# Attention scores in three 64-row passes, two heads side by side in the array

## The chip, the cores and the metric

The kernel runs on one core of a Trainium2 chip. The metric is the device time in microseconds of one execution. Three executions of the kernel before took 2763.01, 2763.8 and 2765.96 us; the median is 2763.8 us.

## What is computed

One layer of a hybrid encoder trunk over 2048 tokens of width 1024, in fp32. The input is normalised and projected; three mixers run in parallel on the projection (chunked attention with 6 heads of 64, a causal depthwise convolution, a retention with 6 heads of 64); their outputs are projected and added, and a squared-ReLU MLP and a gated per-layer embedding follow. The change touches the attention scores:

```python
q = rmsnorm(to_chunk_heads(q, H_ATT), qn_g)
k = rmsnorm(to_chunk_heads(k, H_ATT), kn_g)
...
scores = jnp.einsum('bhncd,bhnkd->bhnck', q, kb).astype(jnp.float32) * (d ** -0.5)
scores = scores + bias[None, :, None]
scores = jnp.where(valid[None, None, :, None, :], scores, -1e30)
probs = jax.nn.softmax(scores, axis=-1).astype(v.dtype)
out = jnp.einsum('bhnck,bhnkd->bhncd', probs, vb)
```

Each query chunk of 64 sees its own chunk and the 8 before it.

## The kernel before

The tokens go through in four blocks of 512 (`T`), block by block through all stages. The weight products run in `float32r`, each operand split into a high part (rounded copy, made by ACT) and a low part (the rest, made by DVE); a product is three matmuls, high x high, high x low, low x high (`mm3s`, L173). Transposes and the smaller products of attention and retention are plain fp32 matmuls.

The order of PE's work is the program's order (`keep_in_program_order`, L54 and L59). It is made by a planner at build time. The main stream is a list of segments (L787 on): convolution projection, gate of the block before, then for each of three head pairs an attention projection (`ap`, 96 matmuls of 384 columns) and a retention projection (`rp`, 96 matmuls of 512 columns), then the output projection (`wo_a`, `wo_b`) and the MLP. `posn` counts the main stream. Into it, `advance` (L844) inserts two chains of side work. Chain 0 holds `att_mix(p)` for each head pair, which begins at a fraction `AS` of `rp` of its pair (L835); chain 1 holds `conv_mix` and `ret_mix(p)`. A chain's step may say for how long PE shall do other work before the next step; that is measured on `clk`, a model of PE time that `PE.matmul` adds up, and the amounts stand in `W` (L261): after the q/k transposes `qk`, after the scores `st`, after the transposes of the scores `ts`. The order on the other engines is set by a scheduler from priorities.

`att_mix(p)` (L428) is run 12 times, once for each block and head pair:

- 8 transposes put q and k of the pair into the PSUM tile `qkT`: 128 rows (two heads of 64) by 512 tokens, for q and for k (L437). They read `an`, the normalised rows that POOL writes (L416) at the end of the attention projection.
- The split (L438 to L447). For each head, q is copied by ACT twice: once as the high part into that head's 64 rows of `q[h]`, once more into the other 64 rows; DVE writes the low part into 64 rows of `qlz[h]`, whose other rows are zero. For k, ACT writes the high part into the head's rows of `k[h]` and DVE the low part into the other rows. That is six ACT and four DVE operations of 64x512.
- `scores(t, h)` (L458) for each tile `t` of 128 queries and head `h`: with q high in both halves and k high and low in the halves, one matmul over 128 rows gives high x high + high x low, and a second with `qlz` gives low x high. The keys lie in two segments, this block's (`k`, 128(t+1) columns) and the block before's (`kprev`, the remaining columns up to 640; block 0 has none). The result `sc` is one of two PSUM buffers of tag `s` (`sb2`, L105). DVE adds the bias and takes the maximum (L472), ACT the exponential (L474).
- `trans` (L478) transposes the probabilities back into the same `sc` buffer; ACT (head 0, L484) and DVE (head 1, L486) copy them out as `pT`, which frees the buffer for the next scores.
- `values` (L489) multiplies with v, the two heads writing 64 output rows each of `po` (L495): PE's stationary operand has 64 columns there.

`both(t)` (L500) issues the scores of both heads; it is called once before the tile loop and then after each tile's transposes. `ret_proj` (L535) evacuates each of its four accumulators with four ACT copies (L550 to L554), and two accumulators (`accb`, L102) alternate. `ret_mix` ends with the transposes `roT` (L637).

Of the kernel before, what the change touches and what calls it, by code (L numbers as in the profile page):

```python
# [12 lines left out]
F32R = mybir.dt.float32r  # L13
AF = mybir.ActivationFunctionType
ALU = mybir.AluOpType
AX = mybir.AxisListType

P = 128
D = 1024
S = 2048  # L20
T = 512
# [3 lines left out]
HD = 64  # L25
# [15 lines left out]
def trunk(ctx, tc, a, out):  # L41
    nc = tc.nc
    V, A, G = nc.vector, nc.scalar, nc.gpsimd
    clk, posn = [0.0], [0.0]

    class PE:
        @staticmethod
        def matmul(o, x, y, start, stop):
            n = y.shape[-1]
            if y.dtype == F32R:  # L50
                clk[0] += max(n, 240) / 2200.0
            else:
                clk[0] += max(4 * n * x.shape[-1] / P, 240) / 2200.0
            tc.keep_in_program_order(nc.tensor.matmul(o, x, y, start=start, stop=stop))  # L54
# [12 lines left out]
    def ctile(name, shape, src=None, dt=F32):  # L67
        t = cpool.tile(shape, dt, tag=name, name=name)
        if src is not None:
            nc.sync.dma_start(t, src)  # L70
        return t

    def stile(tag, bufs, shape, name=None, dt=F32):
        return sp.tile(list(shape), dt, tag=tag, name=name or tag, bufs=bufs)
# [16 lines left out]
    def tmp(name, n):  # L91
        return stile("t", 4, [P, n], name)

    def kv(name, shape=(P, 512), dt=F32):
        return stile("kv", 17, shape, name, dt)
# [9 lines left out]
    def sb2(name):  # L105
        return ps.tile([P, 1024], F32, tag="s", name=name, bufs=2)
# [8 lines left out]
    def pob(name):  # L115
        return ps.tile([P, T], F32, tag="po", name=name, bufs=1)

    def f(t):
        return t.bitcast(F32)
# [81 lines left out]
    def split_tr(b, hi, lo, scale):  # L201
        A.activation(hi, b, AF.Copy, scale=scale)
        V.scalar_tensor_tensor(lo, b, scale, f(hi), ALU.mult, ALU.subtract)
# [54 lines left out]
        A.activation(r, b[:, :T], AF.Copy)  # L258

    cur = {}  # L260
    W = dict(qk=6.0, st=4.5, ts=2.0, vo=1.6, r0=3.5, r1=2.4, r2=1.8, r3=11, c1=3.5, c2=2.6, c3=0.6)  # L261

    def xnorm(blk):
        xh, xl = big("xh", 0), big("xl", 1)
# [87 lines left out]
    def conv_mix():  # L352
# [3 lines left out]
        for u in range(2):  # L356
# [13 lines left out]
            for i in range(2):  # L370
                V.tensor_scalar(z[u][:, i * DC : i * DC + DC], b2[:, i], s6[:, 12 + 2 * i : 13 + 2 * i],
                                s6[:, 18 + i : 19 + i], ALU.subtract, ALU.mult)
            yield W["c1"]
        hl = []
        for c in range(2):
# [7 lines left out]
            hl.append((yh, yl))  # L383
            yield W["c2"]
        yield W["c3"]
        for c in range(2):
# [8 lines left out]
            V.scalar_tensor_tensor(ml[:, c], b, bias, f(mh[:, c]), ALU.add, ALU.subtract)  # L395
            yield W["c2"]

# [25 lines left out]
    def mix():  # L423
        if "m" not in cur:
            cur["m"] = big("mh", 2), big("ml", 3)
        return cur["m"]

    def att_mix(p):  # L428
        nats, v = cur["an", p], cur["v", p]
        kprev, vprev = kvc[p]  # L430
        hs = slice(0, HD), slice(HD, P)
        q = [kv("q", dt=F32R) for _ in range(2)]
        k = [kv("k", dt=F32R) for _ in range(2)]
        b = sb2("qkT")
        for j in range(2):
            for t in range(NT):
                PE.transpose(b[:, j * T + t * P : j * T + t * P + P], nats[t][:, j * P : j * P + P], ident)  # L437
        for j, gain in enumerate((qg, kg)):  # L438
            for h in range(2):
                x, y = hs[h], hs[1 - h]  # L440
                bj = b[x, j * T : j * T + T]
                hi = (q, k)[j][h][x]
                A.activation(hi, bj, AF.Copy, scale=gain[x, 0:1])
                lo = qlz[h][x] if j == 0 else k[h][y]
                V.scalar_tensor_tensor(lo, bj, gain[x, 0:1], f(hi), ALU.mult, ALU.subtract)  # L445
                if j == 0:
                    A.activation(q[h][y], bj, AF.Copy, scale=gain[x, 0:1])  # L447
        yield W["qk"]
        rs = stile("rs", 2, [P, 16])
        bias = []  # L450
        for h in range(2):
            bt = stile("bias", 2, [P, 640])
            with tc.high_priority(offset=200):
                nc.sync.dma_start(bt, a["bias"][2 * p + h])
            bias.append(bt)
        po = pob("po")

        def scores(t, h):  # L458
            x = slice(t * P, t * P + P)
            s = sb2("sc")  # L460
            c0 = t * P if kprev is not None else 512
            c1 = 512 + (t + 1) * P
            segs = [(k, 0, 512, c1 - 512)]
            if kprev is not None:
                segs.append((kprev, c0, c0, 512 - c0))
            for kk, ko, so, n in segs:
                PE.matmul(s[:, so : so + n], q[h][:, x], kk[h][:, ko : ko + n], start=True, stop=False)
                PE.matmul(s[:, so : so + n], qlz[h][:, x], kk[h][:, ko : ko + n], start=False, stop=True)
            n = c1 - c0
            pt = tmp("pt", 640)  # L470
            nm = stile("nm", 3, [P, 1])
            V.tensor_tensor_reduce(pt[:, :n], s[:, c0:c1], bias[h][:, 640 - n :], -1.0, 3e38,  # L472
                                   ALU.add, ALU.min, nm[:, 0:1])
            A.activation(pt[:, :n], pt[:, :n], AF.Exp, bias=nm[:, 0:1], scale=-1.0,  # L474
                         accum_out=rs[:, 2 * t + h : 2 * t + h + 1])
            return s, pt, c0 // P, n // P

        def trans(t, h, s, pt, g0, nch):  # L478
            n = nch * P
            for c in range(nch):  # L480
                PE.transpose(s[:, c * P : c * P + P], pt[:, c * P : c * P + P], ident)
            pT = tmp("pT", 640)
            if h == 0:
                A.activation(pT[:, :n], s[:, :n], AF.Copy)  # L484
            else:
                V.tensor_copy(pT[:, :n], s[:, :n])  # L486
            return pT

        def values(t, pT, g0, nch):  # L489
            for c in range(nch):  # L490
                g = g0 + c
                vv = vprev[:, g] if g < 4 else v[:, g - 4]
                for h in range(2):
                    hr = slice(h * HD, h * HD + HD)
                    PE.matmul(po[hr, t * P : t * P + P], vv[:, hr], pT[h][:, c * P : c * P + P],  # L495
                              start=(c == 0), stop=(c == nch - 1))

        sc = {}

        def both(t):  # L500
            for h in range(2):
                sc[h] = scores(t, h)
            return clk[0] + W["st"]

        rdy = both(0)
        pT = span = None
        for t in range(NT):
            yield rdy - clk[0]
            if t:
                values(t - 1, pT, *span)  # L510
            pT = [trans(t, h, *sc[h]) for h in range(2)]
            span = sc[0][2:]
            yield W["ts"]
            if t < NT - 1:
                rdy = both(t + 1)
        V.reciprocal(rs[:, 8:16], rs[:, 0:8])
        rb = tmp("rb", T).rearrange("p (t n) -> p t n", n=P)
        V.tensor_copy(rb.rearrange("p t (h d) -> p (t h) d", d=HD),
                      rs[:, 8:16].unsqueeze(2).to_broadcast([P, 8, HD]))
        yield W["vo"]  # L520
        b = sb2("rT")
        for i in range(NT):
            PE.transpose(b[:, i * P : i * P + P], rb[:, i], ident)
        rT = tmp("rT", T)
        A.activation(rT, b[:, :T], AF.Copy)
        values(NT - 1, pT, *span)
        yield 0
        kvc[p] = k, v
        mh, ml = mix()
        V.tensor_tensor(rT, po, rT, ALU.mult)  # L530
        A.activation(mh[:, AT[p]], rT, AF.Copy)
        V.tensor_tensor(ml[:, AT[p]], rT, f(mh[:, AT[p]]), ALU.subtract)
        yield 0
# [244 lines left out]
    segs, start = [], {}  # L778
# [24 lines left out]
        seg(("gate", NB - 1, half), lambda half=half: gate(NB - 1, half), cP + 8 * cost(512))  # L803

    tasks = []
    AS, RS, RT0, CS, CE, RE, LE, LF, NE, NF, GE, GF, AS0, CS0, CE0 = 0.25, 0.35, 0.03, 0.4, 0.5, 0.95, 0.4, 0.7, 0.4, 0.55, 0.16, 0.22, 0.25, 0.5, 0.5

    def at(name, frac):
        s, c = start[name]
# [73 lines left out]
    for c in range(2):  # L883
        with tc.high_priority(offset=AHEAD):
            next(first)
        x = slice(c * HALF, c * HALF + HALF)
# [13 lines left out]
    qg = ctile("qg", [P, 1], a["qn_g"])  # L900
    V.tensor_scalar(qg, qg, HD ** -0.5, None, ALU.mult)
    kg = ctile("kg", [P, 1], a["kn_g"])
# [7 lines left out]
    G.memset(hist, 0.0)  # L910
    qz = ctile("qz", [P, NT, 2, P])
    G.memset(qz, 0.0)
    qlz = [ctile(f"qlz{h}", [P, T], dt=F32R) for h in range(2)]
    for h in range(2):
        G.memset(f(qlz[h])[HD - h * HD : P - h * HD], 0.0)
    st = []
    for p in range(NPAIR):
        st.append([ctile(f"st{p}{i}", [P, P]) for i in range(2)])
# [100 lines left out]
```

## Time and profile before

| | before |
|---|---|
| median of 3 runs | 2763.8 us |
| profiled execution, its own time | 2768.22 us |
| its span, first to last instruction | 2766.4 us |
| mean granted TensorE clock | 0.990 |
| PE busy | 2683.5 us, 97% |
| DVE busy | 1344.3 us, 49% |
| ACT busy | 745.3 us, 27% |
| POOL busy | 717.6 us, 26% |

The durations come from one profiled execution, 4.4 us above the median. PE is the matmul row; PEld are the loads of the stationary operand. A matmul's own duration is longer than the distance to the next one's start, since matmuls are pipelined; the pace of PE is read from start to start. The granted clock is that of TensorE as a share of 2.4 GHz; it is 1.00 or 0.50.

### The profile page before, as it was taken

The numbers are of one execution on the slowest core, as the hardware profiler recorded it, in microseconds if no ns is written. First come the engines' busy times: TensorE is split into PE (matmuls) and PEld (weight loads), VectorE is DVE, ScalarE is ACT, GpSimd is POOL, SyncE is SP. The second block draws the span as 40 slices with busy tenths as digits, with TensorE's granted clock in tenths as the row PEclk, the third lists the DMA queues.
The fourth block names the chain that finished last, engine by engine and source line by source line (L and its number), as shares of the span: only waits on it lengthen the run. The fifth ranks groups of instructions, "written<-read, shape, count | busy, mean of one in ns | idle before, by whom it ended". The sixth has DMA issues, their size and how long they took to land.

```text
span 2766.4 us, 34253 instructions
## 1 busy us (share of the span) xinstructions
PE 2683.5 (97%) x13178; PEld 2236.1 (81%) x13178; DVE 1344.3 (49%) x2297; ACT 745.3 (27%) x1506; POOL 717.6 (26%) x676
## 2 busy tenths in 40 slices
PE   7899999999899999999999999999999999999999
PEld 6777788887788888888888888888887888888887
DVE  5966655457745543334664554222376555322222
ACT  4454322234144321112324432000122442100011
POOL 4334534334312231222322213001022221210112
PEclk9999999999999999999999999999999999999999
DMA  7647664656633566767663345555655344555554
GB/s 270 237 146 259 230 215 170 208 176 219 206 121 128 193 212 231 259 222 261 240 208 116 132 156 210 187 194 195 231 191 178 117 151 160 190 192 189 197 195 147
DMA packets 123281, 535.35 MB, mean 194 GB/s; under 512 B 12784, under 2 KB 38128, under 8 KB 77040
## 3 DMA queue, kind: packets, MB, share of 16 engines
q1 hardware_dynamic: 123120, 533.17, 54.7%
q8 instruction: 104, 1.70, 0.3%
q14 instruction: 57, 0.47, 0.1%
HBM read 412.54 MB, written 120.59 MB: 193 GB/s over the span
## 4 chain that ended last, share of the span: by engine, by line
PE 82%; DVE 8%; DMA 4%; ACT 2%; issue 2%; POOL 1%; SPq 0%; DVEq 0%; ACTq 0%; POOLq 0%
PE acc L54 46%; PE w L54 26%; DVE y L340 4%; PE po L54 2%; PE sc L54 2%; PE sc L59 2%; DMA w<-k_wr 1%; PE rout L54 1%; DVE w L127 1%; PE ple L54 1%; PE rsc L54 1%; DMA w<-k_wa 1%; DVE k L445 1%; ACT q L447 0%; DMA raw<-in_wc_dram 0%
## 5 line engine op out<-in xcount | busy, mean ns | idle before, releaser
L54 PE MATMUL acc<-xh,w 128*128 128x512 f32 (+1 forms) x1744 | 549.1, 391 | 8.3 <-DVE gate L768 4.0
L54 PE MATMUL acc<-w,xh 128*128 128x512 f32 (+1 forms) x1536 | 469.0, 380 | 18.0 <-DMA w<-k_wa 6.7
L54 PEld LDWEIGHTS acc<-xh,w 128*128 128x128 f32 x1744 | 327.0, 188 | 80.0 <-issue 5.2
L54 PE MATMUL acc<-hid,w 128*128 128x512 f32 x1536 | 367.0, 392 | 0.0
L54 PE MATMUL w<-hid,w 128*128 128x512 f32 x1536 | 362.0, 391 | 0.0
L54 PEld LDWEIGHTS acc<-hid,w 128*128 128x128 f32 x1536 | 288.4, 188 | 63.6
L54 PEld LDWEIGHTS w<-hid,w 128*128 128x128 f32 x1536 | 288.5, 188 | 63.1
L54 PEld LDWEIGHTS acc<-w,xh 128*128 128x128 f32 x1536 | 287.8, 194 | 61.1 <-DMA w<-k_wr 9.5
L54 PE MATMUL acc<-xl,w 128*128 128x512 f32 (+1 forms) x872 | 335.0, 389 | 0.9 <-DVE xl L234 0.9
L54 PE MATMUL w<-xh,w 128*128 128x512 f32 x1024 | 322.0, 390 | 0.0
L127 POOL TENSOR_TENSOR w<-raw,w 128x512 fp32r<-128x512 f32 (+1 forms) x141 | 186.7, 1325 | 506.3 <-ACT w L126 486.6
L692 POOL TENSOR_TENSOR s<-r 128x512 f32<-128x512 f32 x128 | 157.7, 1233 | 554.9 <-DVE r L691 554.9
L126 ACT ACTIVATE w<-raw 128x512 fp32r<-128x512 f32 (+1 forms) x284 | 160.9, 614 | 498.1 <-PE acc L54 279.6
L54 PE MATMUL acc<-w,xl 128*128 128x384 f32 (+1 forms) x768 | 289.2, 377 | 0.0
L693 ACT ACTIVATE hid<-r 128x512 fp32r<-128x512 f32 x128 | 80.2, 628 | 576.3 <-DVE r L691 576.3
L54 PEld LDWEIGHTS w<-xh,w 128*128 128x128 f32 x1024 | 191.9, 188 | 39.7
L127 DVE TENSOR_TENSOR w<-raw,w 128x512 fp32r<-128x512 f32 (+1 forms) x143 | 180.5, 1263 | 81.9 <-ACT w L126 76.7
L340 DVE SCALAR_TENSOR_TENSOR y<-gl,cw,y 128x512 f32<-128x512 f32 x240 | 207.4, 893 | 2.5
L54 PE MATMUL w<-xl,w 128*128 128x512 f32 x512 | 199.2, 389 | 0.0
L54 PEld LDWEIGHTS acc<-xl,w 128*128 128x128 f32 x872 | 164.2, 188 | 36.1 <-DVE xl L234 1.3
L718 DVE TENSOR_TENSOR h<-h,w 128x512 f32<-128x512 f32 x128 | 87.9, 688 | 197.4 <-PE w L54 196.6
L718 DVE TENSOR_TENSOR h<-h,acc 128x512 f32<-128x512 f32 x128 | 87.8, 687 | 173.3 <-PE acc L54 172.8
(182 smaller groups left out, 3291.2 us busy)
## 6 DMA issues: line engine op xcount, KB each, us to landing
w<-k_w SPq DMA_DIRECT2D x160, 1024.0 KB, 4.8
k_w<-w SPq DMA_DIRECT2D x64, 1024.0 KB, 6.8
raw<-in_w_dram SPq DMA_DIRECT2D x96, 512.0 KB, 4.5
w<-k_wr SPq DMA_DIRECT2D x36, 1024.0 KB, 5.9
w<-k_w_g SPq DMA_DIRECT2D x30, 1024.0 KB, 4.8
w<-k_wa SPq DMA_DIRECT2D x36, 768.0 KB, 6.0
w<-k_w_oa SPq DMA_DIRECT2D x18, 1024.0 KB, 6.1
k_wr<-w SPq DMA_DIRECT2D x12, 1024.0 KB, 7.0
```

Source lines behind the costliest of these rows:

```text
L54: tc.keep_in_program_order(nc.tensor.matmul(o, x, y, start=start, stop=stop))
L59: tc.keep_in_program_order(nc.tensor.transpose(o, x, i))
L126: A.activation(w[:, 0, :n], x, AF.Copy)
L127: eng.tensor_tensor(w[:, 1, :n], x, f(w[:, 0, :n]), ALU.subtract)
L340: V.scalar_tensor_tensor(y, gl[:, j : j + T], cw[:, c, j : j + 1], y, ALU.mult, ALU.add)
L445: V.scalar_tensor_tensor(lo, bj, gain[x, 0:1], f(hi), ALU.mult, ALU.subtract)
L692: G.tensor_tensor(s, r, r, ALU.mult)
L693: A.activation(hid[:, j], r, AF.Square)
L718: V.tensor_tensor(h[j], h[j], b, ALU.add)
```

## The change

q and k each become two tiles of all 128 rows, high and low, with head 0 in rows 0 to 63 and head 1 in rows 64 to 127. One ACT copy and one DVE subtraction of 128x512 make each pair (`split_tr`). Scores of both heads are issued together: for each segment three passes, high x high, high x low, low x high, each pass one 64-row matmul for head 0 and one for head 1, into two score buffers. `qlz` and its memsets go. The planner counts a 64-row matmul as half, waits 5.0 in place of 6.0 after the q/k transposes, and begins the attention chain at 0.4 of `rp` in place of 0.25.

```diff
             if y.dtype == F32R:
-                clk[0] += max(n, 240) / 2200.0
+                clk[0] += max(n, 240) / 2200.0 * x.shape[0] / P
...
-    W = dict(qk=6.0, st=4.5, ts=2.0, vo=1.6, r0=3.5, r1=2.4, r2=1.8, r3=11, c1=3.5, c2=2.6, c3=0.6)
+    W = dict(qk=5.0, st=4.5, ts=2.0, vo=1.6, r0=3.5, r1=2.4, r2=1.8, r3=11, c1=3.5, c2=2.6, c3=0.6)
...
-        for j, gain in enumerate((qg, kg)):
-            for h in range(2):
-                x, y = hs[h], hs[1 - h]
-                bj = b[x, j * T : j * T + T]
-                hi = (q, k)[j][h][x]
-                A.activation(hi, bj, AF.Copy, scale=gain[x, 0:1])
-                lo = qlz[h][x] if j == 0 else k[h][y]
-                V.scalar_tensor_tensor(lo, bj, gain[x, 0:1], f(hi), ALU.mult, ALU.subtract)
-                if j == 0:
-                    A.activation(q[h][y], bj, AF.Copy, scale=gain[x, 0:1])
+        for j, (x, gain) in enumerate(((q, qg), (k, kg))):
+            split_tr(b[:, j * T : j * T + T], x[0], x[1], gain[:, 0:1])
...
-        def scores(t, h):
+        def scores(t):
             x = slice(t * P, t * P + P)
-            s = sb2("sc")
+            ss = [sb2("sc") for _ in range(2)]
...
             for kk, ko, so, n in segs:
-                PE.matmul(s[:, so : so + n], q[h][:, x], kk[h][:, ko : ko + n], start=True, stop=False)
-                PE.matmul(s[:, so : so + n], qlz[h][:, x], kk[h][:, ko : ko + n], start=False, stop=True)
+                for i, (a_, b_) in enumerate(((0, 0), (0, 1), (1, 0))):
+                    for h in range(2):
+                        PE.matmul(ss[h][:, so : so + n], q[a_][hs[h], x], kk[b_][hs[h], ko : ko + n],
+                                  start=(i == 0), stop=(i == 2))
             n = c1 - c0
-            pt = tmp("pt", 640)
...
+            out = []
+            for h, s in enumerate(ss):
+                pt = tmp("pt", 640)
...
+                out.append((s, pt, c0 // P, n // P))
+            return out
...
         def both(t):
-            for h in range(2):
-                sc[h] = scores(t, h)
+            sc[:] = scores(t)
             return clk[0] + W["st"]
...
-    AS, RS, RT0, CS, CE, RE, LE, LF, NE, NF, GE, GF, AS0, CS0, CE0 = 0.25, 0.35, 0.03, 0.4, 0.5, 0.95, 0.4, 0.7, 0.4, 0.55, 0.16, 0.22, 0.25, 0.5, 0.5
+    AS, RS, RT0, CS, CE, RE, LE, LF, NE, NF, GE, GF, AS0, CS0, CE0 = 0.4, 0.35, 0.03, 0.4, 0.5, 0.95, 0.4, 0.7, 0.4, 0.55, 0.16, 0.22, 0.4, 0.5, 0.5
...
-    qlz = [ctile(f"qlz{h}", [P, T], dt=F32R) for h in range(2)]
-    for h in range(2):
-        G.memset(f(qlz[h])[HD - h * HD : P - h * HD], 0.0)
```

The function that the split now calls:

```python
def split_tr(b, hi, lo, scale):
    A.activation(hi, b, AF.Copy, scale=scale)
    V.scalar_tensor_tensor(lo, b, scale, f(hi), ALU.mult, ALU.subtract)
```

How the order moves, in block 1, second head pair. PE before, the end of the work behind the q/k transposes and the first scores of tile 0 (24 matmuls `acc` and the four `roT` stand between `qkT` and the first `sc`):

```order
L59 MATMUL qkT<-ident,an 128x128 x8
L59 MATMUL roT<-ident,ro 128x128 x4
L54 MATMUL acc<-w,xh 128x512
L54 MATMUL acc<-w,xl 128x512
...
L54 MATMUL acc<-w,xh 128x512
L54 MATMUL sc<-k,q 128x128
L54 MATMUL sc<-k,qlz_199 128x128
L54 MATMUL sc<-k,q 128x512
L54 MATMUL sc<-k,qlz_199 128x512
L54 MATMUL sc<-k,q 128x128
```

PE now, the same place (22 matmuls `acc` between `qkT` and `sc`):

```order
L59 MATMUL roT<-ident,ro 128x128 x4
L54 MATMUL acc<-w,xh 128x512
L54 MATMUL acc<-w,xl 128x512
L59 MATMUL qkT<-ident,an 128x128 x8
...
L54 MATMUL acc<-w,xh 128x512
L54 MATMUL sc<-k,q 128x128 x6
L54 MATMUL sc<-k,q 128x512 x6
L54 MATMUL acc<-w,xh 128x512
```

The q/k transposes now stand behind the retention's `roT`, and six matmuls over both heads stand where each head had two of its own.

DVE before, the same head pair, from the first low part of q to the first bias-and-maximum of the scores:

```order
L445 SCALAR_TENSOR_TENSOR qlz_199<-qkT,qg,q 64x512
L203 SCALAR_TENSOR_TENSOR ml<-roT,gng,mh 128x512
L445 SCALAR_TENSOR_TENSOR qlz_200<-qkT,qg,q 64x512
L558 TENSOR_TENSOR rb<-rqk,cs 128x4x32
L559 TENSOR_TENSOR rb<-rqk,cs 128x4x32
L560 TENSOR_TENSOR rn<-rqk,cs 128x256
L445 SCALAR_TENSOR_TENSOR k<-qkT,kg,k 64x512
L565 TENSOR_SCALAR e<-e 128x128
L566 RECIPROCAL e<-e 128x128
L445 SCALAR_TENSOR_TENSOR k<-qkT,kg,k 64x512
L472 ISA pt,nm<-sc,bias 128x640
```

DVE now, the same place:

```order
L203 SCALAR_TENSOR_TENSOR ml<-roT,gng,mh 128x512
L203 SCALAR_TENSOR_TENSOR q<-qkT,qg,q 128x512
L203 SCALAR_TENSOR_TENSOR k<-qkT,kg,k 128x512
L554 TENSOR_TENSOR rb<-rqk,cs 128x4x32
L555 TENSOR_TENSOR rb<-rqk,cs 128x4x32
L556 TENSOR_TENSOR rn<-rqk,cs 128x256
L561 TENSOR_SCALAR e<-e 128x128
L562 RECIPROCAL e<-e 128x128
L468 ISA pt,nm<-sc,bias 128x640
```

Two splits stand one behind the other, and the retention's operations (L554 to L562, before L558 to L566) come behind them.

ACT before, the same place:

```order
L443 ACTIVATE q<-qkT,qg 64x512
L202 ACTIVATE mh<-roT,gng 128x512
L447 ACTIVATE q<-qkT,qg 64x512
L443 ACTIVATE q<-qkT,qg 64x512
L550 ACTIVATE rqk<-acc,xss 128x256
L553 ACTIVATE rn<-acc,xss 128x64 x2
L554 ACTIVATE rn<-acc,xss 128x128
L447 ACTIVATE q<-qkT,qg 64x512
L443 ACTIVATE k<-qkT,kg 64x512
L564 ACTIVATE e<-rn 128x128
L443 ACTIVATE k<-qkT,kg 64x512
```

ACT now:

```order
L560 ACTIVATE e<-rn 128x128
L202 ACTIVATE mh<-roT,gng 128x512
L202 ACTIVATE q<-qkT,qg 128x512
L202 ACTIVATE k<-qkT,kg 128x512
L546 ACTIVATE rqk<-acc,xss 128x256
L549 ACTIVATE rn<-acc,xss 128x64 x2
```

The evacuation of a retention accumulator (`rqk`, `rn`) stood between the copies of q and k; now both copies stand between two evacuations.

## Rows read from the trace of the kernel before

**Rows 1.** The page, part 1: busy us (share of the span) and instructions by engine.
```profile
PE 2683.5 (97%) x13178; PEld 2236.1 (81%) x13178; DVE 1344.3 (49%) x2297; ACT 745.3 (27%) x1506; POOL 717.6 (26%) x676
```

**Rows 2.** Waits of PE: engine, line, waited for; us in total, times, longest.
```profile
PE sc L54 <- DVE k L445: 21.6, 22, 2.6
PE qkT L59 <- POOL an L416: 10.2, 4, 6.6
PE acc L54 <- DMA w<-k_wa: 6.7, 3, 5.3
...
PE acc L54 <- DMA w<-k_wr: 2.6, 4, 1.4
...
PE sc L54 <- DVE pT L486: 1.4, 1, 1.4
```

**Rows 3.** Timeline, PE, block 1, second head pair: start us, us, instruction, [idle before].
```profile
842.06 1.03 PE L59 MATMUL qkT<-ident,an 128*128 128x128 f32 x8
...
849.45 0.33 PE L54 MATMUL sc<-k,q 128*128 128x128 f32 x1 [0.32 <-DVE k L445]
849.61 0.27 PE L54 MATMUL sc<-k,qlz 128*128 128x128 f32 x1
849.72 0.45 PE L54 MATMUL sc<-k,q 128*128 128x512 f32 x1
...
851.48 0.33 PE L54 MATMUL sc<-k,q 128*128 128x128 f32 x1 [1.08 <-DVE k L445]
...
852.73 0.62 PE L54 MATMUL acc<-w,xh 128*128 128x512 f32 x2
853.19 0.39 PE L54 MATMUL acc<-w,xl 128*128 128x512 f32 x1
...
860.00 0.28 PE L54 MATMUL sc<-k,q 128*128 128x256 f32 x1
860.12 0.28 PE L54 MATMUL sc<-k,qlz 128*128 128x256 f32 x1
860.24 0.34 PE L54 MATMUL sc<-k,q 128*128 128x384 f32 x1
860.41 0.34 PE L54 MATMUL sc<-k,qlz 128*128 128x384 f32 x1
```

**Rows 4.** Timeline, ACT and DVE, same head pair: first q copy, last k split.
```profile
843.13 0.69 ACT L443 ACTIVATE q<-qkT,qg 64x512 fp32r<-64x512 f32 x1 [6.30 <-PE qkT L59]
...
850.67 0.76 DVE L445 SCALAR_TENSOR_TENSOR k<-qkT,kg,k 64x512 fp32r<-64x512 f32 x1
```

**Rows 5.** Windows: stretch, us, busy PE PEld DVE ACT POOL, granted clock, DMA, GB/s.
```profile
784.50:787.90 3.40, 3.40 (x9) 2.82 (x10) 1.61 (x4) 1.80 (x4) 0.00 (x0) 0.50 0.00 0
...
2143.00:2146.40 3.40, 3.40 (x10) 2.69 (x9) 1.96 (x5) 1.74 (x4) 0.00 (x0) 0.50 0.00 0
```

**Rows 6.** Groups by form: a split of 128x512 on DVE; busy us, mean ns.
```profile
L203 DVE SCALAR_TENSOR_TENSOR ml<-roT,gng,mh 128x512 fp32r<-128x512 f32 x12 | 8.9, 745 | 14.5 <-ACT mh L202 14.5
```

**Rows 7.** Groups by form: score matmuls of the widest and the narrowest segment.
```profile
L54 PE MATMUL sc<-k,q 128*128 128x512 f32 x42 | 18.8, 447 | 0.0
...
L54 PE MATMUL sc<-k,q 128*128 128x128 f32 x42 | 12.3, 294 | 21.6 <-DVE k L445 21.6
```

**Rows 8.** Timeline, PE, two bursts of the value product and what surrounds them.
```profile
830.78 1.31 PE L54 MATMUL po<-pT,v 128*64 128x128 f32 x20
832.02 0.44 PE L54 MATMUL acc<-w,xh 128*128 128x384 f32 x1
832.30 0.34 PE L54 MATMUL acc<-w,xl 128*128 128x384 f32 x1
...
865.29 0.51 PE L54 MATMUL acc<-w,xh 128*128 128x384 f32 x2
865.73 1.31 PE L54 MATMUL po<-pT,v 128*64 128x128 f32 x20
866.97 1.31 PE L59 MATMUL sc<-ident,pt 128*128 128x128 f32 x10
868.04 0.42 PE L54 MATMUL acc<-w,xl 128*128 128x384 f32 x1
```

More of the change, by code (lines that the diff above doesn't have):

```diff
@@ L466, in scores @@
             for kk, ko, so, n in segs:
-                PE.matmul(s[:, so : so + n], q[h][:, x], kk[h][:, ko : ko + n], start=True, stop=False)
-                PE.matmul(s[:, so : so + n], qlz[h][:, x], kk[h][:, ko : ko + n], start=False, stop=True)
+                for i, (a_, b_) in enumerate(((0, 0), (0, 1), (1, 0))):
+                    for h in range(2):
+                        PE.matmul(ss[h][:, so : so + n], q[a_][hs[h], x], kk[b_][hs[h], ko : ko + n],
+                                  start=(i == 0), stop=(i == 2))
             n = c1 - c0
-            pt = tmp("pt", 640)
[L471 to L476, printed above, removed]
+            out = []
+            for h, s in enumerate(ss):
+                pt = tmp("pt", 640)
+                nm = stile("nm", 3, [P, 1])
+                V.tensor_tensor_reduce(pt[:, :n], s[:, c0:c1], bias[h][:, 640 - n :], -1.0, 3e38,
+                                       ALU.add, ALU.min, nm[:, 0:1])
+                A.activation(pt[:, :n], pt[:, :n], AF.Exp, bias=nm[:, 0:1], scale=-1.0,
+                             accum_out=rs[:, 2 * t + h : 2 * t + h + 1])
+                out.append((s, pt, c0 // P, n // P))
+            return out
         def trans(t, h, s, pt, g0, nch):
@@ L496, in values @@
                               start=(c == 0), stop=(c == nch - 1))
-        sc = {}
+        sc = []
         def both(t):
-            for h in range(2):
-                sc[h] = scores(t, h)
+            sc[:] = scores(t)
             return clk[0] + W["st"]
```

## The prediction

> **What bounds the kernel.** I read the totals first, then PE's waits, then the stretches in which they lie. PE is busy 97% of the span [rows 1], so only two things are worth time: fewer microseconds of array work, and the waits of PE itself. DVE, ACT and POOL at or below 49% cost nothing except where PE stands still for them. The list of PE's waits [rows 2] is short. Its longest entry is PE before a score matmul, waiting for the DVE split of k (L445): 21.6 us in 22 waits. The next is the q/k transposes waiting for POOL's normalised rows (L416): 10.2 us in four. Waits for weight transfers come to 9.3 us, and a wait of scores for the DVE copy of transposed scores happened once, 1.4 us.
>
> One chain shows why the k wait exists [rows 3, 4]. The transposes start at 842.06 us, and scores follow at 849.45 and, for the second head, at 851.48, both times held. ACT's first q copy starts at 843.13, and DVE's last k split at 850.67 ends at 851.43: 8.3 us for six ACT and four DVE operations that wait on each other in turn, with retention work between them. PE's other work covers only part of that.
>
> A wait also costs afterwards. In several stretches right behind such waits the granted clock is 0.50 [rows 5], the lower level, 1.2 GHz. PE's busy time there is twice what it would be at the upper.
>
> **Part 1, the split (four operations for ten).** The price of one does not fall with the partitions: a 64x512 split takes 0.76 us [rows 4], the same operation on 128x512 0.745 [rows 6]. Hence q copy 0.69, q split 0.75, and k split 0.75 (k's copy runs beside q's split): 2.2 us from transposes to last split. Behind the transposes PE now has 22 matmuls of 0.23 us [rows 3], 5.0 us, before the first score. In the changed order no other DVE operation stands between the two splits in blocks 1 to 3. So I cost the k wait there at nothing; its cover is that 2.8 us margin, and without it each chain would wait the overrun. PE's k waits of chains 4 to 12 sum to 16.3 of the 21.6 us and go entirely. Block 0 has 5.3, where DVE is loaded with convolution taps and weight splits, some of them still between the two splits; I credit 4. **-20.3 us.** DVE and ACT themselves get 18 and 33 us lighter (12 chains times 2 and 4 operations of about 0.7 us), worth nothing directly. The two POOL memsets dropped at the start lie before the POOL splits; nothing.
>
> **Part 2, the later start.** AS moves from 0.25 to 0.4 of a retention projection of 96 matmuls: 0.15 x 96 x 0.23 = 3.3 us. Of the four qkT waits (6.6, 2.3, 0.8, 0.5 us), at most 3.1 of the first and all of the rest fit, 6.7. Retention's transposes roT, which stood behind them in two chains of block 0, now come closer and can take about 1.3 back. **-5.4 us.** The start also leaves ACT's q and k copies in the gap between two evacuations of the projection, not across one, so I charge no wait for an accumulator. At the other end, in the changed order some 85 matmuls of 0.23 us still stand between the last head pair's last value product and the projection that reads it, so a start 3 us later does no harm. The SP queue keeps its order in blocks 1 to 3; the bias loads sit at the same place.
>
> **Part 3, the clock.** In blocks 1 to 3 four 0.50 stretches start with or behind k waits (first and last in rows 5), with 16.6 us of PE busy time, of which half, 8.3, comes back if the waits go. In block 0 the stretches behind k and qkT waits hold 19.6; other waits stay there, so I credit 3 of the possible 9.8. **-11.3 us.**
>
> **Part 4, the array.** Start-to-start, score matmuls of 128, 256, 384 and 512 columns take 0.11, 0.12, 0.17 and 0.23 us [rows 3]: 0.63 for a set of the four widths. There are 42 of each width for q [rows 7] and as many for the low part, so 21 sets of four: 4 x 0.63 = 2.52 us each. Three passes of head pairs cost 3 x 0.63 = 1.89 if a pair takes the time of one: 21 x 0.63 = **-13.2 us**. No row has 64-row matmuls, so the pair's price is bounded: 0.63 per set (one) to 1.26 (two in turn). The nearest row is that of the value product, whose two heads use 64 columns each: 20 of them take 1.24 us, against 1.07 for 10 transposes of the same 128-column form [rows 8]. Two halves of the array do run beside each other there, so I take one.
>
> The same rows show what going into and out of halves costs. The two projection matmuls before the burst should end at 865.63, and it starts at 865.73: 0.10 late. The burst takes 1.24 where ten pairs at the transposes' 0.107 would take 1.07: 0.17 more. And the first 384-column matmul behind a burst takes 0.28 where 0.17 is usual: 0.11 [rows 8]. Together 0.38 us a burst. Scores ran with all 128 rows and paid none of it; now there are 48 bursts (12 chains, 4 tiles): 0 to 18.2 us. I take the upper end, as the value product is the only halved work in the trace: **+18.2 us**. So the array work that looks like the gain comes out 5.0 us dearer.
>
> The Trainium skill speaks against this part: "TensorEngine Tiling (Array Packing)", Tiling Modes, says that changing the tiling mode drains the engine, while another tile of the same mode does not. By it row halves would pay as column halves do and the sum stays; were the column rows no guide, it would be the first rival's.
>
> **Part 5, given back.** PE arrives some 2.7 us sooner in each of nine head pairs ((16.3 + 8.3) / 9), while weight buffers come free at the same step. Weight waits are 9.3 us now; I add 3 (bounds 0 to 12.6, one 1.4 us wait in each of nine pairs).
>
> **The sum.** -20.3 - 5.4 - 11.3 - 13.2 + 18.2 + 3 = -29.0 us. The profiled execution took 2768.2 us (span 2766.4), 4.4 over the median of 2763.8: 2768.2 - 29.0 - 4.4 = **2735 us**. About 0.2%, 5.5 us, is what a measurement here can tell from no change.
>
> **The rivals.**
> *Switching is free for row halves.* Then 18.2 us less: 2717. For it: halving by rows leaves the output columns whole, which the value product does not. Against: the only halved rows do pay.
>
> *Weights take turns.* The pitch stops falling below 256 columns (0.11 against 0.12), so something costs 0.11 a matmul whatever it streams. If the two heads' stationary loads go one after the other, a pair costs at least 0.22: a set 3 x (0.22 + 0.22 + 0.22 + 0.23) = 2.67, 0.78 more than forecast, 21 sets: +16.4, 2751. Against it: 20 half-wide products with 20 loads fit into 1.24 us; but those loads are half as long too, so this row does not settle it.
> "TensorE: Matmul & The Clock Gate", LDWEIGHTS, in the Trainium skill says a load's time follows its columns and not its rows, which is this rival's premise; its Part 3 says loads overlap running matmuls of another row group, which is against it.
>
> *Both heads late together.* The first scores of both heads now need both score buffers at once; before, the first head's matmuls ((0.12 + 0.17) x 2 = 0.58 us) covered the DVE copy that frees the second. 36 later tiles x 0.58: +21, 2756. Against: that wait occurred once in 36 [rows 2].
>
> *Not side by side at all (the other side).* If 64-row matmuls go one after another, a set is 6 x 0.63 = 3.78: 1.89 x 21 = 39.7 us dearer than forecast: 2775, slower. It decides from the point where a pair costs 1 + 29.0 / 39.7 = 1.73 of one matmul. For it: no row shows 64-row work, so nothing in the trace excludes it. Against: the column halves overlap.
>
> **How the numbers follow.** Forecast 0.52, free switching 0.20, weights in turn 0.11, both heads late 0.07, not side by side 0.10. The forecast's own spread is about 8 us (k and clock credits of block 0, weight waits). From free switching less 5 to weights in turn plus 3, 2712 to 2754, holds a little over eight in ten. Faster by over 0.2%: the first three and most of the fourth, 0.85; within 0.2%: 0.06, the overlap of late heads and weight waits; slower: 0.09, nearly all from the last rival.
>
> **What would show it.** Right: the row "sc <- DVE k" is gone or under 2 us; no 0.50 clock behind the starts of blocks 1 to 3; score matmuls start two and two, a few ns apart; about 0.1 us lost before a score burst and at the first matmul behind it; qkT waits under 5 us. Wrong: six scores of 512 columns taking 1.4 us and not 0.7; pairs of 128 columns 0.22 apart; new PE waits on pT or acc; the clock dropping at score bursts.

## The result and the profile after

The changed kernel takes 2729.6 us, median of four runs (2726.78 to 2731.06), against 2763.81 for the kernel before on the same chip: ratio 0.9874, 95% interval 0.9857 to 0.9891. The gain is 34.2 us; 29.0 were forecast. The profiled execution took 2730.43 us (span 2728.6).

The page, part 1, answers to [rows 1]:

```profile
PE 2672.2 (98%) x13346; PEld 2218.2 (81%) x13346; DVE 1321.9 (48%) x2273; ACT 712.2 (26%) x1458; POOL 720.7 (26%) x674
```

PE has 168 matmuls more and 11.3 us less busy time; the span is 37.8 us shorter, so most of what went was PE standing still. PE's waits (engine, line, waited for: us, times, longest) answer to [rows 2]:

```profile
PE acc L54 <- DMA w<-k_wa: 7.3, 4, 5.5
PE rkv L54 <- POOL rn L558: 7.0, 4, 3.3
...
PE sc L54 <- DVE pT L483: 2.3, 3, 1.9
...
PE roT L59 <- POOL ro L628: 1.6, 3, 0.5
PE acc L54 <- DMA w<-k_wr: 1.2, 1, 1.2
...
PE sc L54 <- ACT k L202: 0.9, 1, 0.9
PE sc L54 <- DVE k L203: 0.8, 1, 0.8
PE qkT L59 <- POOL an L416: 0.8, 1, 0.8
```

The k wait of 21.6 us is down to 0.8, with 0.9 for ACT's copy of k; the qkT wait of 10.2 is down to 0.8; weights stand at 7.3 + 1.2 = 8.5 for 9.3. The row that grew most is retention's `rkv` product waiting for POOL, 7.0 us for 2.3. Three of its four waits are new and alike, in the third head pair of blocks 1 to 3.

The split of the first pair of block 1, ACT and DVE in order of time, answers to [rows 4]:

```profile
768.69 0.69 ACT L202 ACTIVATE q<-qkT,qg 128x512 fp32r<-128x512 f32 x1 [0.42 <-PE qkT L59]
770.19 0.69 ACT L202 ACTIVATE k<-qkT,kg 128x512 fp32r<-128x512 f32 x1 [0.82 <-DVE q L203]
```
```profile
769.41 0.75 DVE L203 SCALAR_TENSOR_TENSOR q<-qkT,qg,q 128x512 fp32r<-128x512 f32 x1 [0.35 <-ACT q L202]
770.91 0.75 DVE L203 SCALAR_TENSOR_TENSOR k<-qkT,kg,k 128x512 fp32r<-128x512 f32 x1 [0.76 <-ACT k L202]
```

Four operations, 768.69 to 771.66: 2.97 us. k's copy does not run beside q's split; it waits for it. The transposes start at 767.6 and the scores at 773.59, so 1.9 us of the cover are left over.

The stretches at the lower clock level (columns as in [rows 5]) are now these five and a last 0.8 us:

```profile
60.60:64.00 3.40, 3.40 (x9) 2.61 (x9) 3.40 (x5) 0.20 (x1) 1.44 (x1) 0.50 0.62 173
98.20:101.60 3.40, 3.40 (x14) 3.25 (x14) 3.40 (x10) 0.95 (x3) 1.57 (x2) 0.50 0.90 308
135.70:142.60 6.90, 6.08 (x20) 5.14 (x20) 4.49 (x11) 1.61 (x3) 2.57 (x5) 0.51 0.00 1
289.30:292.70 3.40, 3.39 (x8) 2.72 (x9) 3.19 (x2) 0.48 (x1) 3.32 (x3) 0.50 0.31 82
736.50:743.30 6.80, 5.89 (x18) 5.83 (x19) 0.59 (x2) 1.03 (x3) 0.83 (x1) 0.50 0.41 165
...
785.00:787.50 2.50, 2.50 (x15) 2.37 (x14) 1.08 (x4) 2.48 (x8) 0.00 (x0) 1.00 0.94 296
```

Counted like this there were 55.5 us in eleven stretches and a last 0.9 before; now there are 24.7. Both are counts of one execution each. None lies behind an attention start of blocks 1 to 3; 785 us, where one lay before, runs at full clock.

PE's timeline at the first two tiles of that pair (start, us, instruction):

```profile
773.28 0.39 PE L54 MATMUL acc<-w,xh 128*128 128x512 f32 x1
773.59 1.29 PE L54 MATMUL sc<-k,q 64*128 64x128 f32 x12
774.82 0.50 PE L54 MATMUL acc<-w,xh 128*128 128x512 f32 x1
775.15 0.40 PE L54 MATMUL acc<-w,xl 128*128 128x512 f32 x1
...
782.43 0.40 PE L54 MATMUL acc<-w,xl 128*128 128x512 f32 x1
782.76 1.47 PE L54 MATMUL sc<-k,q 64*128 64x256 f32 x12
784.16 0.73 PE L54 MATMUL acc<-w,xh 128*128 128x512 f32 x2
```

Inside the first burst the two heads' matmuls start 3 ns apart, pair behind pair at 0.11 us for 128 columns and 0.23 for 512: the pace of one. The price of switching is at the edges. A full-height matmul of 512 columns takes 0.23, so the burst could start at 773.51 and starts at 773.59; the last pair starts at 774.49 and should be through at 774.72, the next full-height matmul starts at 774.82, and the one behind it 0.33 later and not 0.23.

The second burst shows something new. Its first head starts at 782.76, the second head's first score at 783.08, held for the DVE copy that frees its buffer:

```profile
781.39 0.95 DVE L562 RECIPROCAL e<-e 128x128 f32<-128x128 f32 x1
782.26 0.76 DVE L483 COPY pT<-sc 128x640 f32<-128x640 f32 x1
```

The copy ends at 783.02; it stood behind retention's reciprocal. The list of waits shows little of this, since PE has the first head's matmul running meanwhile.

### The profile page after: what moved, and what is told of

The parts are those of the page before. It is cut to its first block, busy times and chain, and to the rows that moved or that the text cites. A ratio compares the mean times of both kernels' runs of the same rounds, so it can differ in the third digit from the quotient of the medians.

```text
span 2728.6 us, 34532 instructions
## 1 busy us (share of the span) xinstructions
PE 2672.2 (98%) x13346; PEld 2218.2 (81%) x13346; DVE 1321.9 (48%) x2273; ACT 712.2 (26%) x1458; POOL 720.7 (26%) x674
## 4 chain that ended last, share of the span: by engine, by line
PE 84%; DVE 6%; DMA 2%; issue 1%; ACT 1%; POOL 0%; SPq 0%; DVEq 0%; ACTq 0%; POOLq 0%
PE acc L54 48%; PE w L54 26%; DVE y L340 3%; PE po L54 2%; PE sc L54 2%; PE sc L59 2%; PE rout L54 1%; DMA w<-k_wr 1%; PE ple L54 1%; PE rsc L54 1%; DMA w<-k_wa 1%; DVE w L127 1%; PE qkT L59 0%; DVE xl L234 0%; DVE gate L767 0%
## 5 line engine op out<-in xcount | busy, mean ns | idle before, releaser
L54 PE MATMUL acc<-w,xh 128*128 128x512 f32 (+1 forms) x1536 | 463.5, 376 | 16.0 <-DMA w<-k_wa 7.3
L54 PEld LDWEIGHTS acc<-xl,w 128*128 128x128 f32 x872 | 164.9, 189 | 34.8
```

## The experiments

All but one of the eleven runs change an order or a number of the planner. The block lengths given are counted in each trace from the first hidden-layer matmul of one block to that of the next.

**Heads in turn.**

```diff
-                for i, (a_, b_) in enumerate(((0, 0), (0, 1), (1, 0))):
-                    for h in range(2):
+                for h in range(2):
+                    for i, (a_, b_) in enumerate(((0, 0), (0, 1), (1, 0))):
```

> The changed kernel with one thing put differently: within a segment the three passes of the first head are issued, and then the three of the second, so that two matmuls that stand next to each other use the same rows and cannot run side by side. Every count, size and wait stays. Theory (pairs share the array, at the pace of one matmul): a set of four widths goes from 3 x 0.63 to 6 x 0.63 us, 1.89 us for 21 sets, +39.7 us, near 2768; the pages' pitch inside a head would be 0.11 to 0.23 us. Rival A (the array is not what counts, the gain is all waits): within 8 us of the changed kernel, 2722 to 2738. Rival B (the two row halves overlap only in part, as loads do): +10 to +25, 2740 to 2755.

Measured: 2729.86 us, ratio 0.9863 (0.9848 to 0.9878): no difference. That looks like rival A, but the trace shows why it is none: the two heads still start 10 ns apart. How, is best seen in the second tile, where six scores of 256 columns are issued and behind them six of 384. The score matmuls that overlap 785.34 to 785.85:

```profile
L54 PE MATMUL sc<-k,q x5: 275/337/383, 785.3 to 785.8; 64*128 64x256 f32 x4, 64*128 64x384 f32 x1
```

A 384-column matmul of the first head is under way when only four of the six 256-column ones issued ahead of it have started. By these starts the two halves of the rows take their work as two streams, each in its own order. So this run undid nothing, and said nothing about what side by side is worth.

**Both heads on the same rows**, which does undo it:

```diff
-                        PE.matmul(ss[h][:, so : so + n], q[a_][hs[h], x], kk[b_][hs[h], ko : ko + n],
+                        PE.matmul(ss[h][:, so : so + n], q[a_][hs[0], x], kk[b_][hs[0], ko : ko + n],
```

> The changed kernel with both heads' scores taken from the rows of the first head (so the second head's scores are not its own); counts, widths, order and buffers stay. All twelve matmuls of a burst now use the same half of the rows. Heads issued in turn had cost nothing against the changed kernel, and their starts still lay 10 ns apart: the halves seem to take their work as two streams, whatever order it is issued in, so that run did not price side by side. This one does. Theory (one half of the array takes one matmul in the time of a full one, so the pair is worth a factor of two): 21 sets x 1.89 us = +39.7 us, near 2769, between 2762 and 2776, and six 512-column scores take 1.4 us. Rival A (the scores are hidden by what else the tile waits for): under +10, below 2740. Rival B (matmuls of half the rows go faster than full ones even alone): +10 to +25, 2740 to 2755.

Measured: 2764.36 us, ratio 0.9993 (0.9984 to 1.0002): the whole gain is gone. PE's timeline at the first tile of the same pair:

```profile
772.38 0.39 PE L54 MATMUL acc<-w,xh 128*128 128x512 f32 x1
772.70 2.30 PE L54 MATMUL sc<-k,q 64*128 64x128 f32 x12
774.93 0.50 PE L54 MATMUL acc<-w,xh 128*128 128x512 f32 x1
```

The burst lasts 2.23 us from its first start to the next full-height one, for 1.23 in the changed kernel; six scores of 512 columns, 0.23 apart, take 1.4 us. From one pair's transposes to the next it is 65.9 us (766.7 to 832.6) for 62.2 (767.6 to 829.8): 3.7 a chain, where two sets at 1.89 make 3.78. Block 0 gave 1.8 us and not 5.7. Nine chains and block 0: 35 us; the medians lie 34.8 apart, the two traces 32.1. The theory holds, and rivals A and B fall.

**Cover alone**, on the kernel before:

```diff
-    W = dict(qk=6.0, ...
+    W = dict(qk=9.0, ...
```

> The kernel before with one number changed: the work that PE is to have between the q/k transposes and the first score goes from 6 to 9 us. Ten-operation split, two full-height score passes and start of the chain stay. Theory (the gain is k waits and the clock behind them, and cover alone is enough to get it): the k wait of 21.6 us falls to under 4 us, the half-clock stretches behind starts of blocks 1 to 3 go, about 3 us come back at weights: 2764 - 20 - 11 + 3 = 2736, between 2730 and 2743. Rival (the four-operation split matters because of what DVE and ACT are relieved of, or the wait only moves): no more than 10 us are gained, 2754 or above, and a new wait shows on the score transposes or on the accumulators.

Measured: 2738.74 us, ratio 0.99 (0.9885 to 0.9914). The k wait is 1.5 us in two waits:

```profile
PE sc L54 <- DVE k L445: 1.5, 2, 1.3
```

qkT still waits 6.4, and `rkv` waits 7.1 us in four waits, as in the changed kernel. Half clock is 44.8 us, in a profiled execution that took 5.1 us more than the median. One number brings some 28 of the 34 us.

**Old scores, cover and later start**, on the kernel before, run twice (the second time beside the mended kernels below):

```diff
-    W = dict(qk=6.0, ...
+    W = dict(qk=9.0, ...
...
-    AS, ..., AS0, ... = 0.25, ..., 0.25, ...
+    AS, ..., AS0, ... = 0.4, ..., 0.4, ...
```

> The kernel before with its own split and its two full-height score passes, but with 9 instead of 6 us of cover for the split and the later start (0.4 for 0.25). What the change brings in waits is there, the half-height scores are not. Theory (the array part of the change is a small loss, +5 us by the forecast, and the rest of the change comes from order alone): 2764 - 20 - 5 - 11 + 3 = 2730, less what the changed kernel still waits at its second tiles, so 2722 to 2731, as fast as the changed kernel or up to 7 us faster. Rival (half-height pairs are a gain of the size of the saved columns, 13 us, and the ten-operation split brings waits of its own): 2738 to 2750.

> The old scores with 9 us of cover and the later start once more, now on one chip with the mended kernels. Theory: 0.985 of the kernel before again, 2724 to 2728. With the waits gone on both sides the two ways of forming scores stand 2 to 5 us apart in block time by the bursts (5.43 us a chain with row halves where none waits, 5.09 with full rows, times 9, so 3 us), and block 0 goes the other way by some 5 us, so the mended half-row kernel should be 2 to 4 us faster in all. Rival (row halves cost nothing once nothing waits): the mended kernel 6 us faster or more.

Measured: 2726.2 us, ratio 0.985 (0.9837 to 0.9864), and 2726.46, ratio 0.9856 (0.9839 to 0.9872). Without any half-height score the gain is there, at least as large as the changed kernel's. Its blocks 1 to 3 take 683.0 + 667.3 + 668.2 = 2018.5 us (2020.0 in the second run), the changed kernel's 686.5 + 671.0 + 670.8 = 2028.3; block 0 goes the other way by about 5. The same burst with full rows:

```profile
782.03 0.40 PE L54 MATMUL acc<-w,xl 128*128 128x512 f32 x1
782.27 0.22 PE L54 MATMUL sc<-k,q 128*128 128x128 f32 x1
...
783.63 0.62 PE L54 MATMUL acc<-w,xh 128*128 128x512 f32 x2
784.09 0.39 PE L54 MATMUL acc<-w,xl 128*128 128x512 f32 x1
```

It starts with the full-height pace unbroken (782.03 + 0.23) and the pace behind it is 0.23 at once. From the last full-height start ahead to the second behind it is 782.03 to 783.86, 1.83 us; with row halves 773.28 to 775.15, 1.87. Three paired passes against four single ones save 0.34 us here, and the switching takes it back.

**Bursts doubled**: other work may stand between the two segments of a tile's scores.

```diff
                         PE.matmul(ss[h][:, so : so + n], q[a_][hs[h], x], kk[b_][hs[h], ko : ko + n],
                                   start=(i == 0), stop=(i == 2))
+                if kk is not segs[-1][0]:
+                    yield 0
...
-            sc[:] = scores(t)
+            sc[:] = yield from scores(t)
...
-        rdy = both(0)
+        rdy = yield from both(0)
...
-                rdy = both(t + 1)
+                rdy = yield from both(t + 1)
```

> The changed kernel with a point between the two segments of a tile's scores at which other work may be put: in the 36 tiles of blocks 1 to 3 a burst of twelve half-height matmuls becomes two of six with one full-height projection matmul between them. The same matmuls are run. Theory (going into and out of half-height work costs about 0.38 us a burst): 36 more bursts, +13.7 us, 2743; between 2740 and 2747. Rival A (switching is free for row halves, what was read as its cost is the wait of the second head's first score): 2727 to 2733. Rival B (the cost is drained time of the large matmul only, 0.10 us): +3.6 us, 2733.

Measured: 2739.83 us, ratio 0.9903 (0.989 to 0.9917), 10.0 us over the run with heads in turn on the same chip. PE's timeline at the first tile:

```profile
771.46 0.39 PE L54 MATMUL acc<-w,xh 128*128 128x512 f32 x1
771.78 0.55 PE L54 MATMUL sc<-k,q 64*128 64x128 f32 x6
772.26 0.50 PE L54 MATMUL acc<-w,xh 128*128 128x512 f32 x1
772.69 0.96 PE L54 MATMUL sc<-k,q 64*128 64x512 f32 x6
773.58 0.50 PE L54 MATMUL acc<-w,xl 128*128 128x512 f32 x1
773.92 0.62 PE L54 MATMUL acc<-w,xh 128*128 128x512 f32 x2
```

771.46 to 773.92 is 2.46 us; less the 0.23 of the matmul put between and the 1.87 of the undivided burst, 0.36 us for one more burst. 36 of them are 13 us. The total is lower because the second tile's wait shrinks: there the second head starts 0.10 behind the first, for 0.32. So 10.0 lies just under the theory's range (10.4 to 17.4); free switching (rival A) and 0.10 a burst (rival B) do not fit.

**The later start alone**, on the kernel before, and **the start undone**, on the changed kernel, which is the same edit the other way round:

```diff
-    AS, ..., AS0, ... = 0.25, ..., 0.25, ...
+    AS, ..., AS0, ... = 0.4, ..., 0.4, ...
```

> The kernel before with the later start alone (0.4 for 0.25), cover for the split still 6 us. Theory as forecast (qkT waits go, 5.4 us, the k waits of 21.6 us and their half-clock stretches stay): 2758, between 2755 and 2761. Rival A (start and cover stand in for one another: a later start also moves the split away from ACT's and DVE's other work, so part of the k wait goes too): 2742 to 2754. Rival B (with the k wait there the start is worth nothing, the time is waited for k): 2762 to 2766.

Measured: 2767.37 us, ratio 0.9998 (0.9987 to 1.0009): nothing (rival B). The qkT wait is gone and the k wait has taken it up:

```profile
PE sc L54 <- DVE k L445: 26.9, 24, 4.6
```

> The changed kernel with the chain begun where it was begun before (0.25 of the retention projection for 0.4). Everything else stays. Theory as forecast (the later start is worth the qkT waits, 5.4 us): 2735, between 2732 and 2739, with PE's qkT waits back at 6 to 10 us. Rival (the later start is worth what the two runs with the old scores show, 2738.7 against 2726.2, 12.5 us, because what waits at the start is followed by half-clock stretches and by late chains): 2739 to 2745. Second rival (with the four-operation split the start no longer matters): within 2 us of the changed kernel, 2728 to 2732.

Measured: 2734.4 us, ratio 0.9882 (0.9864 to 0.9901), 4.8 us over the changed kernel by the medians. That is the size forecast, but the intervals overlap (0.9857 to 0.9891 for the changed kernel) and the ratios differ by only 2.2 us, so the times alone do not settle it. The qkT wait is back, longer than expected:

```profile
PE qkT L59 <- POOL an L416: 14.0, 6, 6.8
```

All of it is block 0: the stretch up to its hidden layer is 7.4 us longer, and all that follows is 4.2 us shorter together. On the old scores the same step is worth nothing without cover and 12.5 us with it (2738.74 to 2726.2).

**The change mended**, in three forms. The first moves both numbers everywhere, the second in blocks 1 to 3 alone, the third only the one at the tiles, in blocks 1 to 3. The second:

```diff
-            yield W["ts"]
+            yield W["ts"] if kprev is None else 2.5
...
-            chain(1, lambda p=p: ret_mix(p), at(("ap", b, p + 1), RS) if p < 2 else at(("woa", b), RT0),
+            chain(1, lambda p=p: ret_mix(p), at(("ap", b, p + 1), RS) if p < 2 else at(("woa", b), 0.08 if b else RT0),
```

> The changed kernel with two numbers of the order moved: 2.5 for 2.0 us of other work between a tile's score transposes and the next tile's scores, and the retention transposes begun at 0.08 instead of 0.03. Theory (what the changed kernel still loses in each chain is the wait of the second head's first score for the DVE copy of the transposes, about 0.3 us in twelve chains, and the new rkv wait for POOL of 1.4 us in three pairs): -3.5 to -7 us, 2723 to 2726. Rival A (the other half of a chain becomes late instead: a value product or the pair's last projection): 2729 to 2735. Rival B (the 0.3 us is switching, not a wait): 2727 to 2731 with the second tile's burst as long as it is now, 1.6 us.

> The changed kernel with the two numbers of the run before moved in blocks 1 to 3 alone (2.5 us of other work between score transposes and next scores, third pair's retention begun at 0.08 of its projection); block 0 is issued as the changed kernel issues it. The run before had both numbers moved everywhere and came out at the changed kernel's time: by the first hidden-layer matmul of each block its blocks 1 to 3 were 2.8, 2.1 and 2.8 us shorter, and its start up to there 9.5 us longer. Theory (the mend is real and block 0 gave it back): 2729.6 - 7.7 = 2722, between 2720 and 2725, faster than the changed kernel and than the old scores with new cover. Rival A (block 0's length varies by that much on its own, the mend is lost again): 2727 to 2731. Rival B (what comes free in blocks 1 to 3 is waited for at weights): 2726 to 2729 with longer waits for w.

> As the kernel sent with it, without the later start of the third pair's retention. It tells the two halves of the mend apart. Theory: nine chains get 0.33 us back at their second tile (the burst from 1.61 to 1.28 us), 3 us; the three rkv waits of 1.4 us each stay: 2726, between 2724.5 and 2728, some 4 us above the other. Rival (the later tiles take the rkv wait away too, since retention and scores are moved against each other): the same time as the other within 2 us.

Measured, in this order: 2728.71 us (ratio 0.9863, 0.9847 to 0.9879), **2723.15 us** (0.9846, 0.9829 to 0.9863), 2733.09 us (0.9877, 0.9856 to 0.9897). The first missed its theory: it gained in blocks 1 to 3 and gave it back in block 0, where its trace has 34.1 us of half clock for the changed kernel's 17.1. The second shows it: with block 0 as it was, 2723. In the second tile of its first pair all twelve scores now go together:

```profile
782.37 0.62 PE L54 MATMUL acc<-w,xh 128*128 128x512 f32 x2
782.91 1.15 PE L54 MATMUL sc<-k,q 64*128 64x256 f32 x12
783.99 0.50 PE L54 MATMUL acc<-w,xl 128*128 128x512 f32 x1
```

1.08 us to the next full-height matmul, for 1.40. The third missed both its forecasts: it was to be 4 us over the second and is 9.9 by the medians (the intervals just touch). Its `rkv` waits are longer than the changed kernel's, 8.8 us in four, and behind each of the three in blocks 1 to 3 the clock drops (timeline, then windows):

```profile
909.51 0.83 PE L54 MATMUL rkv<-rn 128*128 128x128 f32 x6
912.20 0.52 PE L54 MATMUL rkv<-rn 128*128 128x128 f32 x2 [1.86 <-POOL rn L558]
912.45 1.13 PE L54 MATMUL acc<-mh,w 128*128 128x512 f32 x2
```
```profile
912.50:915.90 3.40, 3.40 (x11) 2.27 (x11) 2.77 (x9) 0.00 (x0) 0.46 (x1) 0.50 0.76 311
1585.00:1588.40 3.40, 3.40 (x13) 2.29 (x13) 2.73 (x9) 0.00 (x0) 0.46 (x1) 0.51 0.72 288
2257.40:2260.80 3.40, 3.40 (x21) 2.56 (x21) 2.00 (x8) 0.00 (x0) 0.46 (x1) 0.50 0.28 116
```

Three stretches of 3.4 us at half pace cost 5.1 at most, and the waits are 4.6 above the second's 4.2: together 9.7 of the 9.9; blocks 1 to 3 of the two traces differ by 9.0. In the changed kernel the same wait, 1.25 us, was followed by full clock (512 columns 0.23 us apart):

```profile
913.33 0.49 PE L54 MATMUL rkv<-rn 128*128 128x128 f32 x2 [1.25 <-POOL rn L558]
914.12 0.39 PE L54 MATMUL acc<-ml,w 128*128 128x512 f32 x1
914.35 0.62 PE L54 MATMUL acc<-mh,w 128*128 128x512 f32 x2
```

The length of a wait does not decide it alone: in the same trace one of 3.29 us, before `rkv` in block 0 at 225.84, was followed by full clock as well.

The second is the fastest kernel of the study, 6.5 us below the changed one by medians, though their intervals still touch (0.9863 against 0.9857). Against the old scores beside it, it is 3.3 us faster, and there the intervals overlap widely: not decided. Its blocks 1 to 3 take 683.3 + 669.2 + 668.3 = 2020.8 us, the old scores' 2018.5 and 2020.0.

## Why the prediction came out right

The range and the side were right, and 29.0 of 34.2 us. The experiments confirm the mechanism: waits and the clock behind them make the gain, the array nothing. How near the total came is in part luck, since some terms erred in opposite directions. Step by step:

- **Part 1, the split: right.** Forecast -20.3; the list of waits gives 21.6 to 1.7, -19.9. One thing in it was wrong: "k's copy runs beside q's split". It waits for it, so the chain is 2.97 and not 2.2 us long; the margin of 2.8 covered that. Cover on the old ten operations does as well, so fewer operations are one way to it and not the only one. In the changed kernel they are the way: its cover, 22 matmuls, is no more than before.
- **Part 2, the later start: right by the rows, too simple in kind.** -5.4 forecast; undoing it costs 4.8 by the medians and 2.2 by the ratios, not clear of noise. The rows give 10.2 to 0.8 for qkT and 1.6 new at `roT`, -7.8 in all. But the term is not additive: the same step gives 0 where the k wait takes up what it saves, and 12.5 us with cover on the old scores.
- **Part 3, the clock: right in blocks 1 to 3, open in block 0.** In blocks 1 to 3 all four stretches behind starts went, as forecast. None of the traces without the k wait has one there, and the later start alone, which keeps the k wait, still has four. In all, half clock fell by 55.5 - 24.7 = 30.8 us, of which half is 15.4, for 11.3; at 0.43 us for 0.23 between 512-column matmuls it is nearer 14. Of the rest, block 0's half clock went from 27.3 to 17.1 us, and half of that fall is 5.1, for the 3 credited. But that is one execution each: three other runs that issue block 0 as the changed kernel does have 17.1, 20.5 and 23.9 us there. And all three have a stretch of 3.4 us near 673 us, which the changed kernel's trace lacks. So it is not shown that the credit was too low.
- **Part 4, the array: right.** Side by side is worth 35 us against 64-row matmuls in turn, and a pair takes the time of one. Switching was put at 0.38 us a burst from the value product; the doubled bursts give 0.36. In blocks 1 to 3 a chain's four bursts take 5.43 us where nothing waits, against 5.09 with full rows: a loss of 0.34 a chain, 3 us in nine. By the block times of the mended kernel it is 0.8 to 2.3 us. Forecast for all twelve was +5.0. The rule of the Trainium skill that was weighed ("TensorEngine Tiling (Array Packing)", Tiling Modes: a change of mode drains the engine, another tile of the same mode does not) agrees with this trace: 0.08 to 0.10 us are lost at either edge of a burst and nothing between the heads. So it backs the term of +18.2; that it speaks against this part, as the prediction has it, is misput.
- **Part 5, given back: wrong place, and the amount near by luck.** Weights did not rise by 3, they fell by 0.8. The wait that rose is `rkv`, by 4.7. I looked for it at the DMA, and it was POOL, which waits for DVE, which waits for ACT's evacuation of an accumulator behind the exponentials of the second tile. Cover alone on the old scores gives three such waits, of 1.0 to 1.2 us for 1.25, so neither the new split nor the half rows are needed for them. That PE arrives sooner at something else's finish is the likely reason; with cover and the later start on the old scores they are not there, so the order has a part in it, and no run takes the two apart.
- **The rivals.** Free switching, weights in turn and not side by side are refuted by the doubled bursts, the pairs' pace of 0.11 and the run on the same rows. Of the loads that spoke against weights in turn, the prediction says that 64 columns are half as long; by their records they take 0.136 us for some 0.19. "Both heads late together" did happen. In blocks 1 to 3 it came once a chain, in the second tile, at 0.32 us (0.60 in one chain) for 0.58, and cost about 3 us, which the mended kernel got back. In block 0 the second head starts 0.13 to 2.33 us late in five of the nine later tiles, 4.0 us together. The list of waits had shown one such wait before, and that list is blind where a first matmul covers the second's wait.

The extra 5 us of gain can't be put down to one term. The terms are read from two executions that lie 37.8 us apart, since the one before was 4.4 us over its median and the one after 0.8. The rows named here make some 32 of that. They do not close better than this: what was read as one chain's wait may be another's cover.

## What to carry to other kernels

Before rebuilding an operation to get a wait off the path, try more cover ahead of the same operation: here one number in the planner gave 28 of 34 us, and with the start moved too, all of it. Matmuls on halves of the rows are as fast as whole ones two at a time, but every change between halves and whole rows costs about 0.36 us a burst; keep such matmuls in few, long bursts. A wait removed is to be looked for at the next thing that PE meets early, and its price is not its length alone: three waits 0.6 us longer were followed by the lower clock here.

## What the runs showed of the hardware

- Matmuls on the two halves of the rows run as two streams: issued three and three, the heads still start 10 ns apart, and one of 384 columns started (785.81 us) ahead of two of 256 columns issued before it (785.89 and 786.01). In the Trainium skill, "TensorE: Matmul & The Clock Gate", Part 3, says that matmuls start and end strictly in program order; the starts in this trace do not agree with that across row halves.
- Half-height matmuls alone are no faster than full ones: 0.11 us for 128 columns, 0.23 for 512.
- A wait of 1.25 us at `rkv` was followed by full clock, one of 1.86 at the same place by 3.4 us of half clock, three times in three. One of 3.29 us in block 0 of the changed kernel was followed by full clock. What else differed ahead of them was not tried.
